# Half of a down projection computed by Strassen's seven products of quarters in a two-layer decoder kernel

## The chip, the cores and the metric

The kernel runs on one core of one Trainium2 chip (trn2). The number of interest is the time of one execution on the device, in microseconds (us). Smaller is better. Beside the times of plain runs there is one execution under the hardware profiler, with a trace of every instruction; durations in this text are from that trace.

The core has a matmul engine (TensorE, PE in the profile; its loads of the stationary operand are listed apart as PEld), a vector engine (VectorE, DVE), a scalar engine (ScalarE, ACT), GpSimd (POOL) and SyncE (SP), which here only issues DMAs. Each engine works through its own queue in order. Matmuls write to PSUM, which has eight banks of 128 x 512 fp32 values here.

## The reference

Two decoder layers on 256 tokens of 1024 features, in float32: a token mixer (forgetting attention in layer 0, block-sparse attention in layer 1), then a SwiGLU feed-forward network (FFN) with 2816 inner features, then a gated per-layer input. The change lies in the FFN alone:

```python
u = _rmsnorm(h, ffn_norm_g[i])
gu = u @ ffn_w_in[i]
h = h + (jax.nn.silu(gu[..., :D_FF]) * gu[..., D_FF:]) @ ffn_w_out[i]
```

The last product is the down projection: (256 tokens x 2816) times (2816 x 1024).

## The kernel before

Activations are held with features on the 128 partitions and the 256 tokens along the free axis. A product in float32 precision is made of three matmuls in a faster 32-bit type (fp32r): every operand x is split into hi = x rounded to fp32r and lo = x - hi, and `mm3` adds hi·hi, hi·lo and lo·hi into one PSUM region. So each weight tile takes a step on ScalarE (`whi`, a copy that rounds, L186) and one on VectorE (`wlo`, a subtraction, L187) after its DMA has filled `raw`. Weights come in blocks of 128 x 1024, numbered in the order of their use (`raw82` is the 83rd); they lie in DRAM in that order. `raw`, `whi` and `wlo` each have a ring of six buffers.

`half` and `blocks` fetch and split one block; `blocks` puts it APART = 16 columns (64 bytes) behind the start of its tile. At some calls `blocks` gets a "form", which shifts the first one or two of its eight 128 x 128 pieces by eight columns (`_BOTH1`, `_BOTH2`, used at `AGAIN`, for instance: up with f = 4 and f = 12) and the rest by 64.

`ffn` goes through 22 row blocks f of 128 inner features:

- `up([f])` takes two weight blocks (gate and up) and makes 2 x 8 x 3 = 48 matmuls into a bank `gu`: stationary operand a 128 x 128 piece of the weights, moving operand 256 columns of the normalized activations `g`.
- `gated` reads that bank on VectorE (`gut`, L610), takes Silu on ScalarE, multiplies (L613) and splits the product into `fh` and `fl` (L301, L302).
- `down(f)` takes one weight block (128 rows x 1024 columns) and makes 8 x 3 = 24 matmuls into four banks `fo` (`acc`): two banks for each half `hf` of the output features. Stationary operand a piece of the weights, moving operand `fh` or `fl`.

The loop runs in pairs: up(f), up(f+1), down(f-2), down(f-1). The last four row blocks are taken by `last`, one half of the output after the other, so that the first half is finished early: it is added to the residual `hx` (its tile is named `gx` in the profile) by `residual(0, ...)` while the second is still running. Between them stands `ple_up` (`pu`), the up product of the per-layer input; in layer 1 its roles are swapped (stationary activations, moving weights), and `by_token` adds f32 transposes (`tp`).

The code is written in program order, and a scheduler then places each instruction in its engine's queue: a split is moved ahead of work whose operands come later, so VectorE and ScalarE run some blocks ahead of TensorE. What limits this lead is the rings: a split waits until TensorE has finished with the block that had its buffer, and a load until VectorE has split the block that was there.

Of the kernel before, what the change touches and what calls it, by code (L numbers as in the profile page):

```python
# [10 lines left out]
F32 = mybir.dt.float32  # L11
F32R = mybir.dt.float32r
# [9 lines left out]
NP = H // 2  # L22
DFF = 2816
FT = DFF // P
DP = 256
EPS = 1e-6
BUCKETS = 32
# [52 lines left out]
def trunk(ctx: ExitStack, tc: tile.TileContext, pt, w, cst, gf, out):  # L80
# [7 lines left out]
    def bank(name):  # L88
        return ps.tile([P, 512], F32, tag="bank", name=name)
# [52 lines left out]
    def half(at=0, entry=0, form=None):  # L142
# [38 lines left out]
        for q in range(parts):  # L181
# [4 lines left out]
            nc.scalar.activation(hi[:, c], raw[:, c], AF.Copy)  # L186
            nc.vector.tensor_tensor(lo[:, c], raw[:, c], f32(hi[:, c]), op=ALU.subtract)  # L187
        return hi, lo

    def blocks(entry=False, form=None):  # L190

# [375 lines left out]
        nf.square(0)  # L567

    def ffn(layer, nm, filler, np_):
        acc = []  # L570
        prod = {}

        def up(fs):

            bks = {f: bank(f"gu{layer}_{f}") for f in fs}

            def step(f, a, wt, k, start):
                o = bks[f][:, a * S:(a + 1) * S]
                if f == a == k == 0:
                    for n, (w_, x) in enumerate(((wt[0][k], nm.k(k)[0]), (wt[1][k], nm.k(k)[0]), (wt[0][k], nm.k(k)[1]))):  # L580
                        mm(o, w_, x, start=n == 0, stop=False, skip_group_check=True)
                else:
                    mm3(o, (wt[0][k], wt[1][k]), nm.k(k), start, k == KT - 1)

            if fs[0] == 0:
                wts = {f: (blocks(form=_BOTH2 if f == 0 else None), blocks()) for f in fs}
                for k in range(KT):
                    if k == 3:
                        nm.turn(1)
                        nm.square(1)  # L590
                    if k == 6:
                        table(AF.Abs_reciprocal_sqrt, nm.ss[:, 0:1])
                    for f in fs:
                        for a in range(2):
                            step(f, a, wts[f][a], k, k == 0 and a == 0)
                nm.root()
                table(AF.Silu, nm.y)
                return fs, bks
            for a in range(2):
                wt = blocks(form=_BOTH1 if (fs[0], a) in AGAIN else None)  # L600
                for k in range(KT):
                    if (fs[0], a, k) == (2, 0, 4):
                        gated(*early)
                    step(fs[0], a, wt, k, k == 0)
            gated(fs, bks)

        def gated(fs, bks):
            for f in fs:
                t = work.tile([P, 2, S], F32, tag="t2k", bufs=3, name=f"gut{layer}_{f}")
                nc.vector.tensor_tensor(t, bks[f].rearrange("p (a s) -> p a s", s=S), nm.rows(), op=ALU.mult)  # L610
                sg = work.tile([P, S], F32, tag="sg", name=f"sg{layer}_{f}")
                nc.scalar.activation(sg, t[:, 0], AF.Silu)
                nc.vector.tensor_tensor(sg, sg, t[:, 1], op=ALU.mult)  # L613
                th = work.tile([P, S], F32R, tag="th", bufs=4, name=f"fh{layer}_{f}")
                tl = work.tile([P, S], F32R, tag="tl", bufs=4, name=f"fl{layer}_{f}")
                split(th, tl, sg)
                prod[f] = th, tl

        def down(f, wt):
            for hf in range(2):  # L620
                feature_unit(acc[hf], wt, 4 * hf, prod[f], f == 0, False)

        def last(f, hf):

            wt = blocks(form={(FT - 2, 0): _BOTH1, (FT - 2, 1): _BOTH1}.get((f, hf)) if layer else None)
            for i in range(2):
                feature_unit(acc[hf], wt, 4 * i, prod[f + i], False, f + i == FT - 1)

        early = up([0, 1])
        for f in range(2, FT, 2):  # L630
            up([f])
            up([f + 1])
            if layer == 0 and f in (6, 8, 10, 12):
                moba[0](f // 2 - 3)
            if f == FT - 6:
                pp = filler()
            if f == 2:
                acc.extend([bank(f"fo{layer}_{hf}_{t}") for t in range(2)] for hf in range(2))
            if f < FT - 2:
                down(f - 2, blocks())  # L640
                down(f - 1, blocks())
        last(FT - 4, 0)
        filler(pp)
        last(FT - 2, 0)
        residual(0, acc[0])
        last(FT - 4, 1)
        np_.turn(0)
        if layer == 0:
            np_.square(0)
        else:  # L650
            by_token(np_, 0)
        last(FT - 2, 1)
        residual(1, acc[1])
# [224 lines left out]
    return t.reshape(2, P, HC).transpose(1, 0, 2).reshape(P, HW)  # L878


def _buckets():
# [78 lines left out]
```

## Time and profile before

| | us |
|---|---|
| median of 3 runs (lowest, highest) | 641.54 (641.27, 641.66) |
| the profiled execution | 641.68 |
| its span, first to last instruction | 639.9 |
| VectorE splits of weight blocks (L187), 198 of them | 237.1 busy |
| ScalarE roundings of weight blocks (L186), 198 | 205.1 busy |

The page's first line gives each engine's busy time and share of the span; a second part cuts the span into 40 slices; a third follows the chain of work that ended last back from the last instruction. Of the answers of the trace, the timeline lists instructions by start (us from the span's start), duration, engine, line, operation, tiles (out<-in) and shape; a row that ends in x8 is eight in a row. The table by windows gives, for stretches of the span, each engine's busy time and number of instructions. TensorE's matmuls overlap: one that is listed with 0.28 us may be followed by the next after 0.11 us, so the spacing of their starts is what counts.

### The profile page before, as it was taken

The numbers are of one execution on the slowest core, as the hardware profiler recorded it, in microseconds if no ns is written. First come the engines' busy times: TensorE is split into PE (matmuls) and PEld (weight loads), VectorE is DVE, ScalarE is ACT, GpSimd is POOL, SyncE is SP. The second block draws the span as 40 slices with busy tenths as digits, with TensorE's granted clock in tenths as the row PEclk, the third lists the DMA queues.
The fourth block names the chain that finished last, engine by engine and source line by source line (L and its number), as shares of the span: only waits on it lengthen the run. The fifth ranks groups of instructions, "written<-read, shape, count | busy, mean of one in ns | idle before, by whom it ended". The sixth has DMA issues, their size and how long they took to land.

```text
span 639.9 us, 13124 instructions
## 1 busy us (share of the span) xinstructions
PE 632.8 (99%) x5300; PEld 611.9 (96%) x5300; DVE 459.2 (72%) x798; ACT 379.4 (59%) x667; POOL 16.3 (3%) x33
## 2 busy tenths in 40 slices
PE   9999999999999999999999999999999999999996
PEld 7899999999999999999989999999999999999985
DVE  6987985886666666658996687678766666666765
ACT  7857675864444445448876486558444444454672
POOL 2500000000000000000000000000000000000002
PEclk9999999999999999999999999999999999999999
DMA  9889744376666666665687544435866566566501
GB/s 333 299 268 362 241 151 148 111 257 198 195 196 196 196 195 206 190 192 167 212 274 261 174 161 149 132 100 180 251 196 198 197 198 194 189 205 194 192 1 66
DMA packets 37212, 125.18 MB, mean 196 GB/s; under 512 B 3968, under 2 KB 7072, under 8 KB 37152
## 3 DMA queue, kind: packets, MB, share of 16 engines
q1 hardware_dynamic: 36832, 123.91, 59.7%
q8 instruction: 41, 0.67, 0.4%
q10 hardware_dynamic: 320, 0.44, 0.2%
q14 instruction: 19, 0.16, 0.1%
HBM read 123.25 MB, written 4.24 MB: 199 GB/s over the span
## 4 chain that ended last, share of the span: by engine, by line
PE 98%; POOL 0%; issue 0%; DVE 0%; ACT 0%; POOLq 0%; DVEq 0%
PE gu L100 12%; PE gu L98 12%; PE gu L99 12%; PE fo L100 6%; PE fo L98 6%; PE fo L99 6%; PE pq L98 5%; PE pq L99 5%; PE pq L100 5%; PE wo L98 2%; PE wo L99 2%; PE wo L100 2%; PE pg L99 2%; PE pg L100 2%; PE pg L98 2%; PE v L98 2%
## 5 line engine op out<-in xcount | busy, mean ns | idle before, releaser
L187 DVE TENSOR_TENSOR wlo<-raw,whi 128x1024 fp32r<-128x1024 f32 (+1 forms) x198 | 237.1, 1202 | 103.8 <-ACT whi L186 101.7
L186 ACT ACTIVATE whi<-raw 128x1024 fp32r<-128x1024 f32 (+1 forms) x198 | 205.1, 1041 | 146.8 <-issue 55.5
L99 PE MATMUL gu<-g,whi 128*128 128x256 f32 x702 | 193.8, 276 | 0.0
L98 PE MATMUL gu<-g,whi 128*128 128x256 f32 x702 | 193.8, 276 | 0.0
L100 PE MATMUL gu<-g,wlo 128*128 128x256 f32 x702 | 193.8, 276 | 0.0
L100 PEld LDWEIGHTS gu<-g,wlo 128*128 128x128 f32 x702 | 131.8, 188 | 0.0
L99 PEld LDWEIGHTS gu<-g,whi 128*128 128x128 f32 x702 | 131.8, 188 | 0.0
L98 PEld LDWEIGHTS gu<-g,whi 128*128 128x128 f32 x702 | 131.8, 188 | 0.0
L98 PE MATMUL fo<-fh,whi 128*128 128x256 f32 x352 | 97.3, 276 | 0.0
L100 PE MATMUL fo<-fh,wlo 128*128 128x256 f32 x352 | 97.2, 276 | 0.0
L99 PE MATMUL fo<-fl,whi 128*128 128x256 f32 x352 | 97.2, 276 | 0.0
L98 PE MATMUL pq<-g,whi 128*128 128x256 f32 x256 | 71.1, 278 | 0.0
L100 PE MATMUL pq<-g,wlo 128*128 128x256 f32 x256 | 70.8, 276 | 0.0
L99 PE MATMUL pq<-g,whi 128*128 128x256 f32 x256 | 70.7, 276 | 0.0
L98 PEld LDWEIGHTS fo<-fh,whi 128*128 128x128 f32 x352 | 66.1, 188 | 0.0
L99 PEld LDWEIGHTS fo<-fl,whi 128*128 128x128 f32 x352 | 66.1, 188 | 0.0
L100 PEld LDWEIGHTS fo<-fh,wlo 128*128 128x128 f32 x352 | 66.1, 188 | 0.0
L98 PEld LDWEIGHTS pq<-g,whi 128*128 128x128 f32 x256 | 48.0, 188 | 1.1 <-issue 0.7
L301 ACT ACTIVATE fh<-sg 128x256 fp32r<-128x256 f32 x44 | 18.1, 416 | 51.6 <-DVE sg L613 51.6
L99 PEld LDWEIGHTS pq<-g,whi 128*128 128x128 f32 x256 | 48.1, 188 | 0.1
L100 PEld LDWEIGHTS pq<-g,wlo 128*128 128x128 f32 x256 | 48.0, 188 | 0.0
L162 ACT ACTIVATE whi<-raw 128x256 fp32r<-128x256 f32 (+3 forms) x44 | 25.4, 623 | 24.0 <-PE pq L99 6.6
(179 smaller groups left out, 984.3 us busy)
## 6 DMA issues: line engine op xcount, KB each, us to landing
raw<-w SPq DMA_DIRECT2D x212, 512.0 KB, 4.2
d<-d SPq DMA_DIRECT2D x4, 768.0 KB, 9.4
raw<-w SPq DMA_DIRECT2D x8, 256.0 KB, 4.5
bias<-d SPq DMA_DIRECT2D x4, 512.0 KB, 7.4
bias<-cd SPq DMA_DIRECT2D x2, 768.0 KB, 8.0
gx<-w SPq DMA_DIRECT2D x1, 512.0 KB, 5.2
bias<-cd SPq DMA_DIRECT2D x1, 512.0 KB, 7.8
p<-pt SPq DMA_DIRECT2D x2, 256.0 KB, 4.3
```

What stands on the lines that cost most here:

```text
L98: mm(o, ah, bh, start=start, stop=False, skip_group_check=True)
L99: mm(o, ah, bl, start=False, stop=False, skip_group_check=True)
L100: return mm(o, al, bh, start=False, stop=stop, skip_group_check=True).ins
L162: nc.scalar.activation(o, raw[:, c], AF.Copy)
L186: nc.scalar.activation(hi[:, c], raw[:, c], AF.Copy)
L187: nc.vector.tensor_tensor(lo[:, c], raw[:, c], f32(hi[:, c]), op=ALU.subtract)
L301: nc.scalar.activation(hi, src, AF.Copy)
```

## The change

For the first 512 output columns (the first half) and the first 18 row blocks (SEVEN = 22 - 4) the down projection is done by Strassen's scheme. A pair of row blocks gives a product of two 2 x 2 matrices of quarters: the activations (two halves of 128 tokens by two row blocks) times the weights (two row blocks by two groups of 256 columns). It takes seven products of quarters where the plain way takes eight, and for them sums of quarters on both sides.

- Weights: `sevenfold` loads the pair's first half as one block (its four quarters in the order that `_quarters` packs), makes four sums on VectorE (`sums`, L197 to L199) in a tile of the `raw` ring, and splits three quarters (128 x 768) and the four sums (128 x 1024). So a pair now takes seven places of each ring, not six. These tiles are used from their start, without APART.
- Activations: `gated` keeps the pair's product in `tt`, and `differences` makes four differences (`dif`, L649 to L651) and splits them into `dh` and `dl`.
- `products`: seven times three matmuls into the four banks `fs` (`seven`), with roles swapped: stationary operand 128 tokens of `fh`, `fl`, `dh` or `dl`, moving operand 256 weight columns. The second half (`acc[1]`) is done as before, with one block for both row blocks.
- After the 18th row block `combined` adds the seven sums (a copy of one bank on ScalarE, five additions on VectorE, tile `c`). The result has tokens on the partitions, so `turned` transposes it (eight 128 x 128 f32 transposes on TensorE into `fc`) between up(20) and up(21) and adds it to the residual. The first half's `acc[0]` starts only with row block 18.

During the loop six PSUM banks are held for sums (four before), so two are left for `gu` (four before). Everything outside the FFN keeps its instructions.

```diff
+SEVEN = FT - 4
...
+    def sevenfold():
...
+        raw, more = [work.tile([P, 4, S], F32, tag="raw", bufs=RAW, name=f"{n}{i}") for n in ("raw", "sums")]
+        nc.sync.dma_start(raw, packed(w, w_at(i), HW))
+        nc.vector.tensor_tensor(more[:, 0:2], raw[:, 1:3], raw[:, 0:1].to_broadcast([P, 2, S]), op=ALU.add)
+        nc.vector.tensor_tensor(more[:, 2], more[:, 0], raw[:, 2], op=ALU.add)
+        nc.vector.tensor_tensor(more[:, 3], more[:, 2], raw[:, 3], op=ALU.add)
+        got = []
+        for q, src in enumerate((raw[:, 1:4], more[:, 0:4])):
+            n = 3 + q
+            hi, lo = [work.tile([P, HW + 2 * LINE], F32R, tag=f"w{x}", bufs=6, name=f"w{x}{i}_{q}")[:, 0:n * S]
+                      .rearrange("p (n s) -> p n s", s=S) for x in ("hi", "lo")]
+            split(hi, lo, src)
+            got += [(hi[:, j], lo[:, j]) for j in range(n)]
+        return got
...
-                th = work.tile([P, S], F32R, tag="th", bufs=4, name=f"fh{layer}_{f}")
-                tl = work.tile([P, S], F32R, tag="tl", bufs=4, name=f"fl{layer}_{f}")
+                th = work.tile([P, S], F32R, tag="e", bufs=6, name=f"fh{layer}_{f}")
+                tl = work.tile([P, S], F32R, tag="pt", bufs=6, name=f"fl{layer}_{f}")
                 split(th, tl, sg)
                 prod[f] = th, tl
-
-        def down(f, wt):
-            for hf in range(2):
-                feature_unit(acc[hf], wt, 4 * hf, prod[f], f == 0, False)
+                if f < SEVEN and f % 2:
+                    differences(f // 2)
+
+        def differences(i):
+            q = quarters.pop(i).rearrange("p k (t s) -> p (k t) s", s=P)
+            d = work.tile([P, 4, P], F32, tag="tt", bufs=3, name=f"dif{layer}_{i}")
+            nc.vector.tensor_tensor(d[:, 0:2], q[:, 2:3].to_broadcast([P, 2, P]), q[:, 0:4:3], op=ALU.subtract)
+            nc.vector.tensor_tensor(d[:, 2], q[:, 3], d[:, 0], op=ALU.subtract)
+            nc.vector.tensor_tensor(d[:, 3], q[:, 1], d[:, 2], op=ALU.subtract)
+            dh, dl = [work.tile([P, 4, P], F32R, tag="qkt", bufs=4, name=f"d{x}{layer}_{i}") for x in "hl"]
+            split(dh, dl, d)
+            diff[i] = dh, dl
+
+        def products(i):
+            b11, b22, b21, x1, x2, x3, x4 = sevenfold()
...
+            for o, at, new, a, b in ((m52, 1, 1, a21, b11), (m43, 0, 1, a22, b21), (m43, 1, 0, a3, b22), (m52, 0, 0, a11, x2),
+                                     (m1, 0, 1, a1, x3), (m76, 1, 1, a6, x1), (m76, 0, 0, a7, x4)):
+                mm3(o[:, at * S:(at + 1) * S], a, b, bool(new) and i == 0, i == SEVEN // 2 - 1)
...
+            nc.scalar.activation(m, m43, AF.Copy)
...
+        def down(f):
+            products(f // 2)
+            wt = blocks()
+            for i in range(2):
+                feature_unit(acc[1], wt, 4 * i, prod[f + i], f + i == 0, False)
...
             up([f])
+            if f > SEVEN:
+                turned(c)
             up([f + 1])
...
             if f < FT - 2:
-                down(f - 2, blocks())
-                down(f - 1, blocks())
+                down(f - 2)
+            if f == SEVEN:
+                c = combined()
```

What the scheduler makes of it is shown at three places in layer 0. The first is TensorE at the first down, right behind up(3). Before, in the first bank `fo0_0_0`, the first two of eight products of row block 0 with weight block 40:

```order
L98 MATMUL fo0_0_0_1809<-fh0_0_1675,whi40_1814 128x256
L99 MATMUL fo0_0_0_1809<-fl0_0_1676,whi40_1814 128x256
L100 MATMUL fo0_0_0_1809<-fh0_0_1675,wlo40_1815 128x256
L98 MATMUL fo0_0_0_1809<-fh0_0_1675,whi40_1814 128x256
L99 MATMUL fo0_0_0_1809<-fl0_0_1676,whi40_1814 128x256
L100 MATMUL fo0_0_0_1809<-fh0_0_1675,wlo40_1815 128x256
```

In the change, from the second of the seven products on: `fs0_0` is the bank m43, `fs0_2` m52, `fs0_1` m1; `w..40_0` are quarters of the weights, `w..40_1` sums of them:

```order
L99 MATMUL fs0_0_1823<-whi40_0_1835,fh0_1_1683 128x256
L100 MATMUL fs0_0_1823<-wlo40_0_1836,fh0_1_1683 128x256
L101 MATMUL fs0_0_1823<-whi40_0_1835,fl0_1_1684 128x256
L99 MATMUL fs0_0_1823<-whi40_0_1835,dh0_0_1691 128x256
L100 MATMUL fs0_0_1823<-wlo40_0_1836,dh0_0_1691 128x256
L99 MATMUL fs0_2_1825<-whi40_1_1839,fh0_0_1675 128x256
L100 MATMUL fs0_2_1825<-wlo40_1_1840,fh0_0_1675 128x256
L101 MATMUL fs0_2_1825<-whi40_1_1839,fl0_0_1676 128x256
L101 MATMUL fs0_0_1823<-whi40_0_1835,dl0_0_1692 128x256
```

The operands have changed places, `dh0_0` is needed from the seventh matmul on, and the first matmul with `dl0_0` has been put three places back, behind a product that needs neither.

The second place is VectorE ahead of these products, from the reading of up(2)'s bank on. Before:

```order
L610 TENSOR_TENSOR gut0_2_1730<-gu0_2_1651,row1_1644 128x512
L302 TENSOR_TENSOR fl0_0_1676<-sg0_0_1672,fh0_0_1675 128x256
L302 TENSOR_TENSOR fl0_1_1685<-sg0_1_1681,fh0_1_1684 128x256
L167 TENSOR_TENSOR wlo42_1876<-raw42_1874,whi42_1875 128x128
L167 TENSOR_TENSOR wlo42_1876<-raw42_1874,whi42_1875 128x896
L613 TENSOR_TENSOR sg0_2_1732<-sg0_2_1732,gut0_2_1730 128x256
L187 TENSOR_TENSOR wlo43_1908<-raw43_1906,whi43_1907 128x1024
```

And with the change, up to the split `dl0_0`:

```order
L629 TENSOR_TENSOR gut0_2_1737<-gu0_2_1651,row1_1644 128x512
L321 TENSOR_TENSOR fl0_0_1676<-tt0_0_1672,fh0_0_1675 128x256
L321 TENSOR_TENSOR fl0_1_1684<-tt0_0_1672,fh0_1_1683 128x256
L649 TENSOR_TENSOR dif0_0_1687<-tt0_0_1672 128x256
L188 TENSOR_TENSOR wlo41_1866<-raw41_1864,whi41_1865 128x1024
L650 TENSOR_TENSOR dif0_0_1687<-tt0_0_1672,dif0_0_1687 128x128
L637 TENSOR_TENSOR tt0_2_1739<-tt0_2_1739,gut0_2_1737 128x256
L651 TENSOR_TENSOR dif0_0_1687<-tt0_0_1672,dif0_0_1687 128x128
L168 TENSOR_TENSOR wlo42_1897<-raw42_1895,whi42_1896 128x128
L168 TENSOR_TENSOR wlo42_1897<-raw42_1895,whi42_1896 128x896
L321 TENSOR_TENSOR dl0_0_1692<-dif0_0_1687,dh0_0_1691 128x512
```

The same work has the differences, the half block 41 and the wait for `dh0_0` between it, and `dl0_0` stands last.

The third is VectorE in the steady part of the loop, around the reading of up(14)'s bank. Before:

```order
L187 TENSOR_TENSOR wlo77_3053<-raw77_3051,whi77_3052 128x1024
L187 TENSOR_TENSOR wlo78_3084<-raw78_3082,whi78_3083 128x1024
L610 TENSOR_TENSOR gut0_14_2942<-gu0_14_2881,row1_1644 128x512
L187 TENSOR_TENSOR wlo79_3114<-raw79_3112,whi79_3113 128x1024
L613 TENSOR_TENSOR sg0_14_2944<-sg0_14_2944,gut0_14_2942 128x256
L302 TENSOR_TENSOR fl0_14_2948<-sg0_14_2944,fh0_14_2947 128x256
L187 TENSOR_TENSOR wlo80_3154<-raw80_3152,whi80_3153 128x1024
L610 TENSOR_TENSOR gut0_15_3012<-gu0_15_2951,row1_1644 128x512
```

With the change, from the split of a set of sums on (`sums76`, of pair 12) to the sums of the next (`sums82`, made from `raw82`):

```order
L321 TENSOR_TENSOR wlo76_1_3120<-sums76_3110,whi76_1_3119 128x1024
L321 TENSOR_TENSOR dl0_6_2893<-dif0_6_2888,dh0_6_2892 128x512
L188 TENSOR_TENSOR wlo77_3146<-raw77_3144,whi77_3145 128x1024
L197 TENSOR_TENSOR sums82_3328<-raw82_3327 128x512
L629 TENSOR_TENSOR gut0_14_3023<-gu0_14_2962,row1_1644 128x512
L188 TENSOR_TENSOR wlo78_3177<-raw78_3175,whi78_3176 128x1024
L637 TENSOR_TENSOR tt0_14_3025<-tt0_14_3025,gut0_14_3023 128x256
L198 TENSOR_TENSOR sums82_3328<-sums82_3328,raw82_3327 128x256
L199 TENSOR_TENSOR sums82_3328<-sums82_3328,raw82_3327 128x256
L321 TENSOR_TENSOR fl0_14_3029<-tt0_14_3025,fh0_14_3028 128x256
```

The first addition on `raw82` now stands between the splits and the reading of the bank; `raw82` is loaded to where `sums76` was, so its load can be issued only when the first row shown is done.

More of the change, by code (lines that the diff above doesn't have):

```diff
@@ L569, in ffn @@
     def ffn(layer, nm, filler, np_):
-        acc = []
-        prod = {}
+        acc, seven = {}, []
+        prod, quarters, diff = {}, {}, {}
         def up(fs):
@@ L610, in gated @@
                 nc.vector.tensor_tensor(t, bks[f].rearrange("p (a s) -> p a s", s=S), nm.rows(), op=ALU.mult)
-                sg = work.tile([P, S], F32, tag="sg", name=f"sg{layer}_{f}")
+                if f >= SEVEN:
+                    sg = work.tile([P, S], F32, tag="sg", name=f"sg{layer}_{f}")
+                else:
+                    if f % 2 == 0:
+                        quarters[f // 2] = work.tile([P, 2, S], F32, tag="tt", bufs=3, name=f"tt{layer}_{f}")
+                    sg = quarters[f // 2][:, f % 2]
@@ new lines, in products @@
+        def products(i):
+            b11, b22, b21, x1, x2, x3, x4 = sevenfold()
+            (a11, a21), (_, a22) = [[[x[:, t * P:(t + 1) * P] for x in prod[2 * i + k]] for t in range(2)] for k in range(2)]
+            a3, a7, a1, a6 = [[x[:, n] for x in diff[i]] for n in range(4)]
+            m43, m1, m52, m76 = seven
+            for o, at, new, a, b in ((m52, 1, 1, a21, b11), (m43, 0, 1, a22, b21), (m43, 1, 0, a3, b22), (m52, 0, 0, a11, x2),
+                                     (m1, 0, 1, a1, x3), (m76, 1, 1, a6, x1), (m76, 0, 0, a7, x4)):
+                mm3(o[:, at * S:(at + 1) * S], a, b, bool(new) and i == 0, i == SEVEN // 2 - 1)
@@ new lines, in combined @@
+        def combined():
+            m43, m1, m52, m76 = [b.rearrange("p (a s) -> p a s", s=S) for b in seven]
+            m = work.tile([P, 2, S], F32, tag="t2k", bufs=3, name=f"m43_{layer}")
+            nc.scalar.activation(m, m43, AF.Copy)
+            c = work.tile([P, 4, S], F32, tag="bias", bufs=1, name=f"c{layer}")
+            nc.vector.tensor_tensor(c[:, 2], m[:, 0], m52[:, 1], op=ALU.add)
+            nc.vector.tensor_tensor(c[:, 1], m[:, 1], m52[:, 0], op=ALU.add)
+            o = c[:, 0:4:3]
+            nc.vector.tensor_tensor(o, m, m52, op=ALU.subtract)
+            nc.vector.tensor_tensor(o, o, m1[:, 0:1].to_broadcast([P, 2, S]), op=ALU.add)
+            nc.vector.tensor_tensor(o, o, m76, op=ALU.add)
+            return c.rearrange("p (t n) s -> p t (n s)", n=2)
@@ new lines, in turned @@
+        def turned(c):
+            bks = [bank(f"fc{layer}_{b}") for b in range(2)]
+            for m in range(4):
+                for t in range(2):
+                    nc.tensor.transpose(bks[m // 2][:, (m % 2) * S + t * P:(m % 2) * S + (t + 1) * P],
+                                        c[:, t, m * P:(m + 1) * P], ident)
+            residual(0, bks)
+        def down(f):
[3 more added lines that the diff above has]
+                feature_unit(acc[1], wt, 4 * i, prod[f + i], f + i == 0, False)
@@ L637, in ffn @@
             if f == 2:
-                acc.extend([bank(f"fo{layer}_{hf}_{t}") for t in range(2)] for hf in range(2))
+                seven.extend(bank(f"fs{layer}_{t}") for t in range(4))
+                acc[1] = [bank(f"fo{layer}_1_{t}") for t in range(2)]
             if f < FT - 2:
-                down(f - 2, blocks())
-                down(f - 1, blocks())
+                down(f - 2)
+            if f == SEVEN:
+                c = combined()
+        acc[0] = [bank(f"fo{layer}_0_{t}") for t in range(2)]
         last(FT - 4, 0)
```

10 lines of the change are left out of this document (7 added, 3 removed).

## The prediction

> **What bounds the kernel now.** I read the page first, its busy line, the slices of the granted clock and the chain that ended last:
>
> ```profile
> PE 632.8 (99%) x5300; PEld 611.9 (96%) x5300; DVE 459.2 (72%) x798; ACT 379.4 (59%) x667; POOL 16.3 (3%) x33
> PEclk9999999999999999999999999999999999999999
> PE 98%; POOL 0%; issue 0%; DVE 0%; ACT 0%; POOLq 0%; DVEq 0%
> ```
>
> TensorE is busy for 632.8 of 639.9 us at full clock, and the chain is TensorE for 98%. A "busy" TensorE says little, so I looked at the starts of its matmuls in the timeline of one pair of row blocks: the first matmul of gu (up), of fo (down) and of the next gu. Then at the same stretch in the table by windows (length, PE busy, instructions, clock, DMA share, GB/s), and at most of layer 0's FFN there, all engines (PE, PEld, DVE, ACT, POOL):
>
> ```profile
> 172.00 0.28 PE L98 MATMUL gu<-g,whi 128*128 128x256 f32 x1
> 182.88 0.28 PE L98 MATMUL fo<-fh,whi 128*128 128x256 f32 x1
> 188.32 0.28 PE L98 MATMUL gu<-g,whi 128*128 128x256 f32 x1
> ...
> 172.00:188.32 16.32, 16.32 (x147) 1.00 0.64 196
> ...
> 139.33:290.00 150.67, 150.67 (x1331) 150.67 (x1330) 94.79 (x112) 72.64 (x97) 0.00 (x0) 1.00 0.64 201
> ```
>
> A pair is 96 matmuls of gu in 10.88 us and 48 of fo in 5.44 us: 0.1133 us from start to start in both, with no hole. So in this stage the time is the number of TensorE instructions times their spacing; VectorE (63%) and ScalarE (48%) lie beside it. Three things can move the end: the number, the spacing, and a new hole.
>
> **What is removed.** Each pair loses a block of three matmuls out of 24 (seven products for eight), in nine pairs of each of two layers: 54 matmuls x 0.1133 = **6.12 us** off the path.
>
> **Turning back.** 16 transposes are new on TensorE (eight in each layer), within up's work. The trace has eight f32 transposes of the same shape amid fo:
>
> ```profile
> 606.21 1.03 PE L701 MATMUL tp<-cs,gx 128*128 128x128 f32 x8
> 607.00 0.36 PE L98 MATMUL fo<-fh,whi 128*128 128x256 f32 x1
> 607.21 0.28 PE L99 MATMUL fo<-fl,whi 128*128 128x256 f32 x1
> ```
>
> From 606.21 to 607.21 stand these eight and one fo matmul; less the latter's 0.113 that is 0.89 us, and some 0.03 for settling: 2 x 0.92 = **+1.84 us**, with 0.05 each way. The Trainium skill ("TensorE: Matmul & The Clock Gate", Part 4: PE-mode transpose) speaks against the change here: about 275 ns a transpose in a kernel's context. By that figure the 16 would take 4.4 us and the whole sum would end 2.6 us later, at an estimated 644.1; the rows give about 0.11 us each, so the trace does not agree.
>
> **The spacing of the products.** In gu and fo the stationary operand is a weight block, set 16 columns (64 bytes) off its tile's start (APART), and the moving one an activation at its tile's start. In the products the roles are swapped and both lie at a start or at whole steps of 512 bytes from it. The nearest rows are pu's and pu_own's 256-wide matmuls, which have the same roles and no offset either; and the wo stretch, which has the old offset and still another spacing:
>
> ```profile
> 600.15 0.28 PE L99 MATMUL pu<-wlo,phi 128*128 128x256 f32 x1
> ...
> 600.75 0.28 PE L98 MATMUL fo<-fh,whi 128*128 128x256 f32 x1
> ...
> 601.34 0.28 PE L100 MATMUL fo<-fh,wlo 128*128 128x256 f32 x1
> ...
> 632.72 0.28 PE L98 MATMUL pu_own<-u,phi 128*128 128x256 f32 x1
> ...
> 633.30 0.28 PE L100 MATMUL pu_own<-u,plo 128*128 128x256 f32 x1
> ...
> 96.00 0.28 PE L98 MATMUL wo<-o,whi 128*128 128x256 f32 x1
> ...
> 96.59 0.29 PE L100 MATMUL wo<-o,wlo 128*128 128x256 f32 x1
> ```
>
> pu: five in 0.60 us, 0.120 each. pu_own: five in 0.58, 0.116. I take 0.118. For 2 x 9 x 21 = 378 products that is 378 x 0.0047 = **+1.8 us** over the old spacing; the ends are 0 (as gu) and +2.5 (all as pu). On the way back from pu the first five fo matmuls took 0.59 (600.75 to 601.34), 0.024 over the old spacing; that settling comes 18 times: **+0.4 us** (0 to 1).
>
> The Trainium skill (same page, Part 2: What happens when you issue a matmul) has a rule by which no such term exists: the moving operand and the weight load each have their own read port, and loading the next weights takes nothing from the running matmul. By it the placement would cost nothing and the sum would be that of the first rival below; pu's 0.120 against gu's 0.113 does not agree.
>
> **The work beside it.** Durations on VectorE overlap, so I take start to start:
>
> ```profile
> 178.68 1.22 DVE L187 TENSOR_TENSOR wlo<-raw,whi 128x1024 fp32r<-128x1024 f32 x1 [0.34 <-ACT whi L186]
> 179.82 0.42 DVE L613 TENSOR_TENSOR sg<-sg,gut 128x256 f32<-128x256 f32 x1
> ...
> 108.81 1.28 DVE L328 TENSOR_TENSOR gx<-gx,wo 128x512 f32<-128x512 f32 x2
> ...
> 130.05 0.75 DVE L613 TENSOR_TENSOR sg<-sg,gut 128x256 f32<-128x256 f32 x2
> ...
> raw<-w SPq DMA_DIRECT2D x212, 512.0 KB, 4.2
> ```
>
> 1024 elements: 1.14; 512: 1.28 less 0.68 = 0.60; 256: 0.33; hence 0.87 for 768 and 0.20 for 128. A pair now costs VectorE 6 x 1.14 + 2 x 0.60 (gut) + 4 x 0.33 = 9.36 us. New per pair: the split of 768 (0.87), sums (0.60 + 0.33 + 0.33), differences (0.33 + 0.20 + 0.20) and their split (0.60), together 3.46: 12.82 of the pair's 15.98 us (141 x 0.1133). ScalarE gains 768 and 512 elements. Both stay beside TensorE. What is queued in order matters more: "sums" takes a place in the ring of six raw tiles, and the load of the next quarters (raw82) goes where sums76 was, so it is issued only when wlo76_1 is done, 4.2 us before it lands; but the first addition on raw82 stands three rows behind wlo76_1, and gut14 and all later splits are queued behind it. The loop from one such split to the next: load 4.2; then 0.60 + 0.60 + 1.14 + 0.33 + 2 x 0.33 + 0.33 + 1.14 for the rest of block 14, 0.60 + 1.14 + 0.33 + 1.14 + 0.33 for 15, and 0.33 + 0.87 + 0.40 + 1.22 up to the end of the split: 11.1 + 4.2 = 15.3 us, some 15.7 with the handovers. TensorE's 15.98 is just longer. VectorE idles some 2 us a pair for the load, and the splits stay ahead: wlo84 stands in the queue before gut17, which waits for the end of w81, and TensorE still has w82 and w83 (about 5 us) before it needs w84. Cost 0; with that cover gone, rival three.
>
> **The first products.** Here the cover is short. TensorE comes to down(0) at 133.88, and now it needs the differences' split, behind much else on VectorE:
>
> ```profile
> 127.71 1.29 DVE L610 TENSOR_TENSOR gut<-gu,row 128x512 f32<-128x512 f32 x2
> 128.91 1.22 DVE L187 TENSOR_TENSOR wlo<-raw,whi 128x1024 fp32r<-128x1024 f32 x1
> ...
> 133.88 0.28 PE L98 MATMUL fo<-fh,whi 128*128 128x256 f32 x1
> ```
>
> gut0 and gut1 end about 128.8 as before (of the three splits ahead of them the last is now a 768). Then in the new order: wlo40_1 1.14, two multiplications 0.66, gut2 0.60, two fl 0.66, differences 0.73 with wlo41 1.14 and a multiplication 0.33 between, wlo42 1.2, dl0 0.69: 7.15 us, so dl0 is there at 136.0. ScalarE's dh0 comes after the last difference (134.1), a 256 and a 512, near 135.0. TensorE does six matmuls (to 134.56), waits 0.45, does five (135.57), waits 0.45: about 1.0 with the semaphores. Layer 1 starts alike: **+2.0 us** (0.8 to 3). From then on the lead grows, since up brings 10.9 us of TensorE before the next products.
>
> **The end of the sums.** combined() waits for the last products. VectorE has two splits, a multiplication, an fl and five additions (2 x 0.33 + 3 x 0.60) before c: about 8 us after w87, and TensorE comes to the transposes 2.5 + 2.72 + 5.44 = 10.6 us after it. ScalarE's copy of m43 waits for the products too, with whi93 and fh19 queued behind it, which TensorE needs only after the transposes. Cost 0 (up to 1 in each layer if a load is late).
>
> **The sum.** -6.12 + 1.84 + 1.8 + 0.4 + 2.0 = -0.1 us on the profiled execution's 641.68 (span 639.9 and 1.8 around it), which is 0.14 above the median of the runs shown. Forecast: **641.5 us**, its own range 639.8 to 643.5. About 0.2% (1.3 us) is what a measurement can tell from no change.
>
> **The rivals.**
> 1. *The products run at gu's spacing* and the return settles at once: -6.12 + 1.84 + 2.0 = -2.3, **639.3**. For it: at the very first 256-wide pu matmul (600.04 to 600.15) the step was still 0.11. Against: the five after it.
> 2. *The slow spacing stays after the products* (the other side). wo shows that a stretch with the old offset can stay at 0.118 (five in 0.59 at 96.00, up to the stretch's end). If fo comes out of the products in this state, gu goes on in it, until something sets it off again: the first block that AGAIN shifts at f = 4 and 12, or the next products. Per layer nine fo of 24, six up pairs of 96 and the 48 before the transposes: 840 matmuls, x 2 x 0.0047 = +7.9, less the 0.4 of settling: **649.0**; some pairs alone give 644 to 648. For it: layer 1's fo at 600.75 came back quickly, but with its first block shifted, which down's blocks() does not ask for. Against: gu, fo and pu change places elsewhere without a trace of it. It decides against the change from a fifth of these matmuls on.
> 3. *VectorE's loop with the load becomes the bound*, if loads take over 5 us: each 0.3 us over the 15.98 eats the lead of some 5 us, and what is left past that in nine pairs twice is +1 to +5: **644**.
> 4. *The first products' wait is hidden too* and the spacing is gu's: **637.4**.
>
> **How the numbers follow.** Forecast 0.42, rival one 0.22, two 0.25, three 0.06, four 0.05. Range 638.8 to 648.5: it holds the forecast, nearly all of rival one, three and most of two, and takes in the unknown spacing from 0 to +2.5 and the wait from 0.8 to 3. Faster by over 0.2%: 0.06 of the forecast, 0.20 of rival one, and four: 0.31. Within: 0.28 and 0.02: 0.30. Slower: 0.08, two and three: 0.39.
>
> **What would show it.** The starts of fs matmuls in a pair well inside: 21 in 2.38 us (rival one) or 2.5; the first gu after the products 0.113 or 0.118 (rival two). In layer 0 a hole on TensorE ahead of the first dh matmul, released by ScalarE, and one ahead of the first dl. fc: eight in about 0.9, without a hole before. VectorE idle ahead of the first addition of sums, ended by the load, but no idle TensorE at whi or wlo inside the stage. I am wrong if TensorE waits there, or if fo and gu change their spacing.

## The result, and the profile after

| | median (us) | lowest to highest | runs |
|---|---|---|---|
| before, beside it | 641.6 | 641.27 to 642.12 | 4 |
| the change | 649.86 | 649.36 to 650.46 | 4 |

The ratio is 1.0128 (95% interval 1.0111 to 1.0146): **slower by 1.3%**, 8.4 us above the forecast and beyond its range. The profiled execution took 649.79 us, its span 648.0.

The page of the change, busy line, slices of the granted clock, chain:

```profile
PE 640.0 (99%) x5262; PEld 617.9 (95%) x5262; DVE 521.5 (80%) x956; ACT 405.3 (63%) x705; POOL 16.3 (3%) x33
PEclk9999999999999999999999999999999999999998
PE 91%; DVE 5%; DMA 1%; issue 1%; ACT 1%; POOL 0%; POOLq 0%; DVEq 0%
```

TensorE has 38 instructions fewer (5300 to 5262: 54 out, 16 in), its busy time is 7.2 us longer, the clock is the same. Fewer instructions and more time means a wider spacing, so again the starts decide. TensorE's timeline of the change, at the borders of one pair inside the stage: the last matmul of gu, the first and the last of fs, the first of fo, and where the next gu begins:

```profile
167.69 0.28 PE L101 MATMUL gu<-g,wlo 128*128 128x256 f32 x1
167.81 0.28 PE L99 MATMUL fs<-whi,fh 128*128 128x256 f32 x1
...
170.21 0.28 PE L101 MATMUL fs<-whi,dl 128*128 128x256 f32 x1
170.32 0.28 PE L99 MATMUL fo<-fh,whi 128*128 128x256 f32 x1
```

The table by windows of the change, cut at such borders (length, busy and instructions of PE, PEld, DVE, ACT, POOL, then clock, DMA share, GB/s; neighbours that reach over a border are counted too): the 96 gu ahead of these products, the 21 products, the 24 fo behind them, and the 96 gu at f = 12:

```profile
156.50:167.81 11.31, 11.31 (x99) 11.31 (x98) 8.87 (x14) 5.38 (x7) 0.00 (x0) 1.00 0.62 202
167.81:170.32 2.51, 2.51 (x23) 2.51 (x22) 2.48 (x5) 2.09 (x3) 0.00 (x0) 1.00 0.65 199
170.32:173.15 2.83, 2.83 (x27) 2.83 (x25) 2.83 (x8) 1.50 (x3) 0.00 (x0) 1.00 0.58 193
206.46:217.36 10.90, 10.90 (x99) 10.90 (x97) 8.02 (x13) 5.29 (x7) 0.00 (x0) 1.00 0.54 188
```

The products step by 0.120 us (2.51 / 21), fo behind them by 0.118 (2.83 / 24), and gu by 0.118 too (11.31 / 96), where it was 0.1133 before. Inside the loop only gu at f = 4 and f = 12, whose first block AGAIN shifts, goes back (10.90 for 96), until the next products. That is rival two. Behind the transposes the two layers differ: in layer 0 gu went back to the quick step without a shifted block (the 47 matmuls behind the first took 5.34 us, 0.114 each), in layer 1 it stayed at 0.118 (5.53). The clock is 1.00 in all of these.

TensorE's waits in the change, and the timeline at the two places in layer 0:

```profile
PE gu L600 <- DVE g L234: 0.5, 2, 0.2
PE fs L101 <- DVE dl L321: 0.4, 2, 0.2
```

```profile
111.83 0.29 PE L600 MATMUL gu<-g,wlo 128*128 128x256 f32 x1
112.35 0.39 PE L600 MATMUL gu<-g,whi 128*128 128x256 f32 x1 [0.24 <-DVE g L234]
112.58 0.28 PE L99 MATMUL gu<-g,whi 128*128 128x256 f32 x1
...
134.76 0.28 PE L101 MATMUL fs<-whi,fl 128*128 128x256 f32 x1
135.11 0.39 PE L99 MATMUL fs<-whi,dh 128*128 128x256 f32 x1
...
135.69 0.28 PE L101 MATMUL fs<-whi,fl 128*128 128x256 f32 x1
136.14 0.39 PE L101 MATMUL fs<-whi,dl 128*128 128x256 f32 x1 [0.17 <-DVE dl L321]
...
278.32 1.04 PE L685 MATMUL fc<-cs,c 128*128 128x128 f32 x8
279.11 0.36 PE L99 MATMUL gu<-g,whi 128*128 128x256 f32 x1
279.32 0.28 PE L100 MATMUL gu<-g,whi 128*128 128x256 f32 x1
```

The steps are 0.52 and 0.23 at the first gu, 0.35 ahead of dh, 0.45 ahead of dl, each of the latter two with a second step of 0.22 behind it. The wait at gu was not in the prediction: the first addition of `sums` stands on VectorE ahead of a residual addition, and the splits of g, which TensorE needs, are queued behind.

Steps from start to start, added up over all TensorE rows of the two traces, give the whole account (us):

```
                                   before    after   difference
54 matmuls fewer, at 0.1133                            -6.1
fs, spacing over 0.1133 (378)                          +2.4
fo, spacing over before's (624)                        +2.1
gu, spacing (2112 matmuls)                             +5.7
first products, waits                                  +1.6
first gu, waits                                        +1.05
fc, 16 transposes and the step behind                  +1.8
sum                                                    +8.5
gu in all                          239.62   246.59     +6.97
fo and fs in all                   119.84   119.70     -0.14
```

Added up before rounding, the differences give 8.4 (6.97 - 0.14 + 1.58 for the 16 transposes themselves). The spans differ by 8.1, since the first matmuls of the program, which wait for loads, took 0.2 less in the execution after.

### The profile page after: what moved, and what is told of

It reads as the page before. It is cut to its first block, busy times and chain, and to the rows that moved or that the text cites. A ratio compares the mean times of both kernels' runs of the same rounds, so it can differ in the third digit from the quotient of the medians.

```text
span 648.0 us, 13258 instructions
## 1 busy us (share of the span) xinstructions
PE 640.0 (99%) x5262; PEld 617.9 (95%) x5262; DVE 521.5 (80%) x956; ACT 405.3 (63%) x705; POOL 16.3 (3%) x33
## 4 chain that ended last, share of the span: by engine, by line
PE 91%; DVE 5%; DMA 1%; issue 1%; ACT 1%; POOL 0%; POOLq 0%; DVEq 0%
PE gu L100 12%; PE gu L101 11%; PE gu L99 11%; PE pq L99 5%; PE pq L101 4%; PE pq L100 4%; PE fo L100 4%; PE fo L99 4%; PE fo L101 4%; PE fs L101 2%; PE fs L99 2%; PE fs L100 2%; PE pg L101 2%; PE pg L100 2%; PE pg L99 2%; PE v L99 2%
## 5 line engine op out<-in xcount | busy, mean ns | idle before, releaser
L188 DVE TENSOR_TENSOR wlo<-raw,whi 128x1024 fp32r<-128x1024 f32 (+1 forms) x180 | 214.4, 1196 | 51.3 <-ACT whi L187 49.4
L187 ACT ACTIVATE whi<-raw 128x1024 fp32r<-128x1024 f32 (+1 forms) x180 | 184.9, 1036 | 101.2 <-PE gu L100 32.7
L99 PE MATMUL gu<-g,whi 128*128 128x256 f32 x702 | 196.2, 279 | 0.0
L100 PE MATMUL gu<-g,whi 128*128 128x256 f32 x702 | 196.0, 279 | 0.0
L99 PE MATMUL fo<-fh,whi 128*128 128x256 f32 x208 | 58.3, 280 | 0.0
L101 PE MATMUL fo<-fh,wlo 128*128 128x256 f32 x208 | 58.2, 280 | 0.0
L100 PE MATMUL fo<-fl,whi 128*128 128x256 f32 x208 | 58.2, 280 | 0.0
L99 PEld LDWEIGHTS fo<-fh,whi 128*128 128x128 f32 x208 | 39.7, 191 | 0.0
L101 PEld LDWEIGHTS fo<-fh,wlo 128*128 128x128 f32 x208 | 39.1, 188 | 0.0
L100 PEld LDWEIGHTS fo<-fl,whi 128*128 128x128 f32 x208 | 39.1, 188 | 0.0
L168 DVE TENSOR_TENSOR wlo<-raw,whi 128x256 fp32r<-128x256 f32 (+3 forms) x44 | 29.3, 683 | 8.9 <-ACT whi L163 8.8
```

Source lines behind the costliest of these rows:

```text
L99: mm(o, ah, bh, start=start, stop=False, skip_group_check=True)
L100: mm(o, ah, bl, start=False, stop=False, skip_group_check=True)
L101: return mm(o, al, bh, start=False, stop=stop, skip_group_check=True).ins
L168: nc.vector.tensor_tensor(t[:, a + b0 * P:a + b1 * P], raw[:, b0 * P:b1 * P], f32(ht[:, a0:a0 + (b1 - b0) * P]), op=ALU.subtract)
```

## The experiments

Theory A: the spacing is set by how the stationary and the moving operand lie to each other; the products leave TensorE in a slow spacing that stays, and a shifted first block ends it. Theory B: the heavier traffic of VectorE and ScalarE beside TensorE slows it. The kernel of before beside the runs had medians of 641.25 to 641.6.

| run | median (us) | lowest to highest | ratio to before (95%) |
|---|---|---|---|
| e1_kick | 647.05 | 645.15 to 648.53 | 1.0093 (1.0076 to 1.0109) |
| e2_apart | 648.06 | 647.92 to 648.79 | 1.0103 (1.0088 to 1.0118) |
| e3_both | 648.10 | 644.6 to 649.71 | 1.0094 (1.006 to 1.0128) |
| e4_flat | 670.18 | one run | |
| e5_ring | 647.94 | 646.38 to 651.77 | 1.0109 (1.0073 to 1.0146) |
| e6_ringonly | 650.37 | 649.94 to 650.51 | 1.0137 (1.012 to 1.0154) |
| e7_start | 648.07 | 646.66 to 648.36 | 1.0098 (1.0083 to 1.0113) |
| e8_step | 651.42 | 648.41 to 652.26 | 1.0146 (1.0121 to 1.0172) |
| e10_queue | 642.80 | 642.65 to 643.26 | 1.0022 (1.0012 to 1.0033) |
| e11_all | 640.45 | 640.2 to 641.32 | 0.999 (0.9981 to 1.0) |
| e12_first | 639.49 | 639.41 to 639.8 | 0.9971 (0.996 to 0.9982) |
| e13_stat | 638.75 | 638.57 to 639.43 | 0.996 (0.9947 to 0.9974) |

### The spacing: e1 to e4

e1, against the change:

```diff
         def down(f):
             products(f // 2)
-            wt = blocks()
+            wt = blocks(form=_BOTH1)
```

> The change, with the first block of fo behind each pair's products read shifted, in the form that AGAIN gives up's blocks at f = 4 and 12 (one argument in down). Nothing else differs. Theory A, rival two of the prediction (the products leave TensorE in a slow spacing, and a shifted block sets it off again): fo and gu step by 0.113 us again in nearly all pairs, the products stay at 0.120, and the time falls by about 840 x 2 x 0.0045 = 7.6 less some 18 x 0.03 for settling, from 649.9 to 642.8 (641.8 to 644). Theory B (what VectorE and ScalarE now read and write beside TensorE slows its matmuls, so the spacing follows the load and not an order of addresses): no change, fo and gu at 0.118, 649.9 within 0.7.

e1, the same three stretches by windows (gu, products, fo):

```profile
156.33:167.21 10.88, 10.88 (x98) 10.88 (x97) 8.79 (x15) 5.48 (x8) 0.00 (x0) 1.00 0.60 201
167.21:169.73 2.52, 2.52 (x23) 2.52 (x22) 2.48 (x5) 1.86 (x3) 0.00 (x0) 1.00 0.53 176
169.73:172.47 2.74, 2.74 (x26) 2.74 (x25) 2.74 (x7) 1.72 (x3) 0.00 (x0) 1.00 0.60 185
```

gu is at 0.1133 again (10.88 / 96), fo at 0.114 with its settling, the products unchanged, with VectorE and ScalarE as busy as before the edit. The spacing did what A says and B does not. The time did not: 2.8 us less instead of 7.1, and its executions lie 3.4 us apart. TensorE had a new wait in layer 1:

```profile
PE fc L685 <- DVE c L677: 2.1, 1, 2.1
PE fs L101 <- DVE dl L321: 1.2, 2, 0.6
```

The first of these stands ahead of the transposes, for the last of `combined`'s additions, and takes back part of the gain. The profiled execution, at 645.15, is the fastest of the four.

e2, against the change (e3 is e1 and e2 together):

```diff
-            hi, lo = [... name=f"w{x}{i}_{q}")[:, 0:n * S]
+            hi, lo = [... name=f"w{x}{i}_{q}")[:, 3 * APART:3 * APART + n * S]
```

> The change, with the split quarters in whi and wlo (the products' moving operand) set 48 columns off the tile's start; pg_own reads an operand with that offset at 0.113 us in the trace. Nothing else differs. Theory A (spacing is set by where the two operands lie): the products step by 0.113 instead of 0.120: 378 x 0.0066 = 2.5 us less, 647.4. If products that run at the quick spacing also leave fo and gu in it, another 7.6: 639.8. Between these two A alone doesn't decide. Theory B (load of the other engines): no change, 649.9 within 0.7.

> Both edits together: the products' moving operand 48 columns off its tile's start, and the first block of fo behind them shifted. Theory A: products, fo and gu all at 0.113 us: 649.9 - 2.5 - 7.6 + 0.5 = 640.3 (639 to 642). Theory B: no change, 649.9 within 0.7.

e2 by windows: products behind a quick gu, fo, slow gu, products behind that:

```profile
151.29:153.77 2.48, 2.48 (x24) 2.48 (x22) 2.42 (x5) 2.34 (x3) 0.00 (x0) 1.00 0.87 274
153.77:156.59 2.82, 2.82 (x26) 2.82 (x25) 2.82 (x6) 1.25 (x3) 0.00 (x0) 1.00 0.84 296
156.59:167.90 11.31, 11.31 (x98) 11.31 (x97) 8.92 (x14) 5.38 (x7) 0.00 (x0) 1.00 0.61 192
167.90:170.31 2.41, 2.41 (x24) 2.41 (x22) 2.38 (x4) 1.99 (x3) 0.00 (x0) 1.00 0.58 201
```

With the offset the products have two spacings too: 0.118 behind a quick gu (2.48 / 21) and 0.115 with settling behind a slow one (2.41 / 21); fo behind them was slow either way. The time fell by 1.8 of the 2.5 named. In e3 fo and gu came back as in e1 but for two stretches of layer 0, which stayed at 0.118 (fo behind the first products, and all from the transposes to the end of its fo), and the wait for c grew to 3.7 us: 640.3 was missed mainly for the same reason as in e1.

e4, against the kernel of before, both places in `blocks`:

```diff
-            return half(APART, 0, form)
-        hi, lo = half(APART, ENTRY * P if entry else 0)
+            return half(0, 0, form)
+        hi, lo = half(0, ENTRY * P if entry else 0)
```

> The kernel of before, no products, with every weight block at its tile's start instead of 16 columns behind it (the form that AGAIN shifts stays shifted). The placement alone, under the old load of VectorE and ScalarE. Theory A: gu, fo and wo step by 0.118 to 0.120 us over most of their length; some 4000 matmuls x 0.005 to 0.0066 = 20 to 26 us slower than before, less what the shifted blocks win back, so 655 to 668. Theory B: no change from 641.6, within 1.

e4 by windows, 48 fo and the 96 gu behind them:

```profile
172.60:178.36 5.76, 5.76 (x51) 5.76 (x49) 3.90 (x5) 2.73 (x4) 0.00 (x0) 1.00 0.60 185
178.36:189.88 11.52, 11.52 (x99) 11.52 (x97) 6.36 (x7) 4.85 (x6) 0.00 (x0) 1.00 0.56 182
```

0.120 us a matmul, without a single product, with the light VectorE of before, and 28.6 us slower in all (one execution). The offset alone makes that difference; B cannot. It is the same 0.120 as that of the products in the change. The time lies 2 us above the expected range, which counted on the shifted blocks to win something back: here they did not, gu at f = 4 took 0.120 too.

### What eats the gain: e5 to e8, e10

In e1 the first addition of each pair's sums waits on VectorE for its load. VectorE's timeline of e1, these rows alone:

```profile
179.50 0.69 DVE L197 TENSOR_TENSOR sums<-raw 128x512 f32<-128x512 f32 x1 [0.70 <-DMA raw<-w]
195.58 0.69 DVE L197 TENSOR_TENSOR sums<-raw 128x512 f32<-128x512 f32 x1 [1.83 <-DMA raw<-w]
212.42 0.69 DVE L197 TENSOR_TENSOR sums<-raw 128x512 f32<-128x512 f32 x1 [2.50 <-DMA raw<-w]
229.64 0.69 DVE L197 TENSOR_TENSOR sums<-raw 128x512 f32<-128x512 f32 x1 [3.53 <-DMA raw<-w]
246.22 0.69 DVE L197 TENSOR_TENSOR sums<-raw 128x512 f32<-128x512 f32 x1 [2.88 <-DMA raw<-w]
```

From one to the next (179.50 to 246.22 in four pairs) are 16.68 us; TensorE in e1 takes 10.88 + 2.52 + 2.74 = 16.14 a pair. So VectorE falls behind by half a us a pair. In the change TensorE's 11.31 + 2.51 + 2.83 = 16.65 just covers it.

That is not all of e1's wait for c. It came in layer 1 alone, though layer 0 has the same loop. In layer 1 ScalarE also stands still for the load of u (weights of the per-layer input, needed later), and there the next rounding, for which VectorE then waits 3.39 us, is queued behind it. ScalarE's timeline at u, in e1 and then in e10, which follows below:

```profile
576.85 0.63 ACT L320 ACTIVATE u<-u 128x512 fp32r<-128x512 f32 x1 [3.61 <-DMA u<-w]
```

```profile
584.82 0.64 ACT L321 ACTIVATE u<-u 128x512 fp32r<-128x512 f32 x1 [1.12 <-DMA u<-w]
```

e5 is e1 with the sums in a tile of their own; e6 has that edit alone:

```diff
-        raw, more = [work.tile([P, 4, S], F32, tag="raw", bufs=RAW, name=f"{n}{i}") for n in ("raw", "sums")]
+        raw, more = [work.tile([P, 4, S], F32, tag=tag, bufs=b, name=f"{n}{i}") for n, tag, b in (("raw", "raw", RAW), ("sums", "bias", 1))]
```

> The change with fo's first block shifted as in the run e1_kick, and besides the tile that holds the sums moved out of the ring of six raw tiles into the space that is free between the attention's bias and c, so that no load of weights waits for a split of sums. In e1_kick the spacing came back as theory A says, but TensorE waited 2.1 us in layer 1 for c, and the lead of the splits over their first use fell by 0.3 to 2 us a pair once a pair took 16.1 us. Theory L (VectorE's loop with the load through the ring takes 16.5 us or more a pair, not the 15.3 to 15.7 of the prediction, so it eats what TensorE gains): without that loop the lead stays at 8 us or more, no wait for c, 643.0 (642.3 to 643.8) with executions within 1 us. Rival U (the late load of u in layer 1, with the splits queued behind it on ScalarE, makes that wait by itself): the lead may stay, but a wait of 1 us or more ahead of fc in layer 1 remains, 645 to 648.

> The change with nothing but the sums' own tile as in the run e5_ring; fo isn't shifted. Theory A with L: TensorE at 0.118 us takes 16.65 us a pair and hides the loop, so nothing moves: 649.9 within 0.7. If part of what the change lost was the ring, the time falls by that part, and the forecast's cost of 0 for the loop was wrong in this kernel already.

e6 moved nothing, as A with L had it. e5 did not move either: 647.94 with a wait of 2.3 us at c is what U named, not L. But neither run tests the loop, since the addition's idle time was as large as before (21.9 us in e6). That the loop is hidden in the change is seen from the change's own trace, where TensorE has no wait inside the stage once the first products are past. All 18 of these additions in the change, in e1 and in e5 (the row by line, then the idle time ahead of them and its count):

```profile
L197 DVE TENSOR_TENSOR sums<-raw x18: 680/692/693, 109.5 to 563.0; 128x512 f32<-128x512 f32 x18
...
  DMA raw<-w: 17.4, 12
```

```profile
L197 DVE TENSOR_TENSOR sums<-raw x18: 678/691/693, 109.4 to 559.2; 128x512 f32<-128x512 f32 x18
...
  DMA raw<-w: 23.2, 12
```

```profile
L197 DVE TENSOR_TENSOR sums<-raw x18: 678/692/695, 109.2 to 558.2; 128x512 f32<-128x512 f32 x18
...
  DMA raw<-w: 24.5, 13
```

With the freer ring the scheduler put the addition one row earlier, and it still stood ahead of its load.

e5's trace shows a second cost of such a wait. Behind it the granted clock fell to 0.50 for some 3 us, and matmuls stepped by 0.21. By windows, from 591.57 on:

```profile
591.57:594.77 3.20, 3.20 (x16) 3.20 (x16) 3.20 (x6) 0.42 (x1) 0.00 (x0) 0.50 0.89 302
```

The traces of e3, e7 and e8 have such a stretch behind each wait for c of 2.3 us or more (3.3 to 3.9 there). e1's, with a wait of 2.1, has none. A stretch like this costs about 1.5 us (15 steps of 0.21 in place of 0.1133, an estimate from e5's rows). It may be why executions of these kernels lie up to 5.4 us apart: e1's profiled one had a mean granted clock of 0.997, its three slower ones 0.995.

e7 mends the starts:

```diff
-                nc.vector.tensor_tensor(self.ss, self.ss, sq, op=ALU.add)
+                self.added = nc.vector.tensor_tensor(self.ss, self.ss, sq, op=ALU.add).ins
...
-        nc.vector.tensor_tensor(more[:, 0:2], raw[:, 1:3], raw[:, 0:1].to_broadcast([P, 2, S]), op=ALU.add)
+        with tc.issue_after(behind) if behind is not None else nullcontext():
+            nc.vector.tensor_tensor(more[:, 0:2], raw[:, 1:3], raw[:, 0:1].to_broadcast([P, 2, S]), op=ALU.add)
...
-                    differences(f // 2)
+                    with nullcontext() if f > 1 else tc.high_priority():
+                        differences(f // 2)
...
-            b11, b22, b21, x1, x2, x3, x4 = sevenfold()
+            b11, b22, b21, x1, x2, x3, x4 = sevenfold(None if i else nm.added)
```

> e5_ring, with two changes of order on VectorE at the start of each FFN: the additions of the first sums stand behind the sums of squares instead of ahead of the residual and g's splits, and the first differences ahead of fl0 and fl1. That removes the waits that the profile of the change shows there: 0.41 and 0.11 at the first matmuls of gu, and 0.23 + 0.11 and 0.34 + 0.11 at the first products, about 1.3 a layer. If these waits are costs of their own: e5_ring less 2.6, so 640.4 if that gives 643.0. If something behind them is as late (the first loads), less than 1 of it shows.

The waits at both starts were gone from its trace, and the wait for c grew from 2.3 to 3.9 us: the gain ahead of the loop was given back behind it, and e5's time did not fall (648.07). e8, on top of e7, has the products' moving operand at `3 * APART + 8 - 8 * q` (q = 0 the quarters, q = 1 the sums):

> e7_start, with the products' moving operand 48 columns off its tile's start for the four sums (as in e2_apart) and 56 for the three quarters, a step of 8 columns at the products' fourth factor and at their first. In e2_apart products that came behind a slow gu ran at 0.114 and behind a quick one at 0.118. If the step sets them off as the shifted block does in gu: products at 0.113 to 0.114, 378 x 0.006 = 2.3 less than e7_start, about 638. If not: 0.118, 0.7 less.

Its products stayed at 0.118 and it was slower, not quicker: layer 0 now waited for c as well (3.3 us, and 3.7 in layer 1). e10 is e1 with one order given, that of the additions in VectorE's queue (by the `issue_after` of e7):

```diff
-                nc.vector.tensor_tensor(sg, sg, t[:, 1], op=ALU.mult)
+                done[f] = nc.vector.tensor_tensor(sg, sg, t[:, 1], op=ALU.mult).ins
...
-            b11, b22, b21, x1, x2, x3, x4 = sevenfold()
+            b11, b22, b21, x1, x2, x3, x4 = sevenfold(done[2 * i + 1] if i else None)
```

> e1_kick with one change of order: the additions of a pair's sums stand on VectorE behind the pair's last multiplication (tt of the odd row block) instead of ahead of gut of the even one. Nothing else, and the sums stay in the ring of raw tiles. In e1_kick and e5_ring VectorE stands idle for 2.1 to 2.4 us a pair at the first of these additions, until the quarters have landed, while gut, whose gu is long done, and the splits are queued behind it; the lead of the splits falls by 0.8 to 1 us a pair and layer 1 ends with TensorE waiting for c. Theory H (that place in the queue makes the loop): no idle VectorE at that addition, the lead stays above 6 us, no wait for c, 643.1 (642.3 to 644) with executions within 1 us. Rival W (VectorE and ScalarE have too much work for 16.1 us a pair, whatever the order): the lead still falls, 645 or more.

e10, the same additions, and VectorE's timeline at two of them and the next gut:

```profile
L198 DVE TENSOR_TENSOR sums<-raw x18: 681/685/693, 109.5 to 566.4; 128x512 f32<-128x512 f32 x18
...
  DMA raw<-w: 0.5, 2
```

```profile
220.31 0.69 DVE L198 TENSOR_TENSOR sums<-raw 128x512 f32<-128x512 f32 x1
...
236.45 0.69 DVE L198 TENSOR_TENSOR sums<-raw 128x512 f32<-128x512 f32 x1
...
242.84 0.69 DVE L630 TENSOR_TENSOR gut<-gu,row 128x512 f32<-128x512 f32 x1 [0.51 <-PE gu L101]
```

0.5 us of idle time instead of 23.2, 16.14 us from one to the next, and VectorE waits for TensorE, not the other way. No wait for c, 642.80 of the 643.1 named, executions within 0.6. W (too much work) does not hold, and in this loop H does. U is not settled: with the new order the scheduler also moved u (the second of the two rows above), 8 us later and behind the roundings that stood behind it in e1, and it waits 1.1 us for 3.6. In e8's layer 0 a wait for c came without any u; how e1's 2.1 us divide between loop and u was not tested.

### Together: e11 to e13

> e7_start (shifted first block of fo, the sums' own tile, the order at the start of each FFN) with the order of e10_queue. Theory H: no wait for c, no wait at the first gu and the first products (e7_start's profile has none left), so e10_queue less 2.4: 640.7 (639.8 to 641.8), even with the kernel of before. Rival W: 644 or more.

640.45: 2.35 less than e10; in the traces the stretches at the two starts are 2.6 shorter. The seven products now break even with the kernel of before. e12 offsets the products' moving operand and sets b11 eight columns further:

```diff
+            for j0, j1, at in ((0, 1, 3 * APART + 8), (1, 3, 3 * APART + LINE)) if q == 0 else ((0, n, 3 * APART),):
```

> e11_all, with the products' moving operand 48 columns off its tile's start and the first factor of the seven (b11) 8 columns further, in its own split: what sets gu off, tried on the products. If it does: products at 0.113 instead of 0.120, 378 x 0.0066 = 2.5 less than e11_all, 638.2. If not, as in e8_step: 0.118, 0.7 less; the two splits more per pair may cost the lead.

639.49, 1.0 less, and the products at 0.118: not set off. e13 shifts a stationary factor instead (moving operand at 3 * APART throughout):

```diff
+            for n0, n1, at in ((0, 1, FURTHER), (1, 4, LINE)):
+                dh, dl = [b[:, at + n0 * P:at + n1 * P].rearrange("p (n s) -> p n s", s=P) for b in both]
+                split(dh, dl, d[:, n0:n1])
```

> e11_all, with the products' moving operand 48 columns off its tile's start and the third factor on the stationary side (a3, first of the differences) 8 columns off the place of the other three: what is shifted in gu and fo is the stationary operand, in e12_first it was the moving one, and there the products stayed at 0.118 from the fourth matmul to the last. If a shifted stationary operand sets them off: some ten of the 21 of a pair, behind a3 and a few of settling, at 0.113: 18 x 10 x 0.0045 = 0.8 less than e12_first, 638.7. If not: 0.118 throughout, 639.5 as e12_first (within 0.4).

e13, products of one pair: the first, the first on the shifted a3 (dh), the second on a11 four matmuls later, the last, and fo:

```profile
182.37 0.28 PE L99 MATMUL fs<-whi,fh 128*128 128x256 f32 x1
...
183.08 0.28 PE L99 MATMUL fs<-whi,dh 128*128 128x256 f32 x1
...
183.56 0.28 PE L100 MATMUL fs<-wlo,fh 128*128 128x256 f32 x1
...
184.69 0.28 PE L101 MATMUL fs<-whi,dl 128*128 128x256 f32 x1
184.81 0.28 PE L99 MATMUL fo<-fh,whi 128*128 128x256 f32 x1
```

Up to 183.56 ten steps take 1.19 us (0.119), from there ten take 1.13 (0.113). Ten of 21 came back, as named, and the time is 638.75 of 638.7: 0.4% below before.

## Why the prediction was wrong

- **The step that failed** is the term "+0.4 us" for settling back, with the "Against" of rival two. It took the way back from `fo` in layer 1 (five slow matmuls), whose first block is shifted, as the way back of down's fo, whose first block is not. The prediction says so itself in rival two, and still gave the quick return more weight. The runs showed that fo and gu go on at 0.118 until something sets them off: the term measured +7.8 (2.1 in fo, 5.7 in gu), and e1's shift alone removed all but some 0.7 of it. That "gu, fo and pu change places elsewhere without a trace of it" was no evidence: between gu and fo no operand changes sides, and the shifted blocks stand where it would have shown.
- **The spacing of the products**: 0.120 rather than 0.118, +2.4 for +1.8, inside its ends. e4 shows the cause that the prediction only argued. The Trainium skill ("TensorE: Matmul & The Clock Gate", Part 2: What happens when you issue a matmul) has two independent read ports and says that loading the next weights takes nothing from the running matmul. The prediction read that as a rule by which no placement would cost anything, and so read it does not agree with e4: 0.120 against 0.1133 with nothing but an offset taken away.
- **The removed matmuls and the transposes** were right: 54 fewer; fc took 0.79 up to the next start plus a step of 0.21 where 0.113 would stand, 0.89 a layer for 0.92, with no hole ahead. One point of the working does not hold: the Trainium skill (same page, Part 4: PE-mode transpose) gives about 275 ns as the duration of one transpose (measured there with bf16), and the trace agrees, since the row of eight lasts 1.04 us and seven steps of 0.109 leave 0.27 for the last. The prediction took the figure as the time from one to the next, and so found a disagreement.
- **The first products**: right in place and order, 0.8 a layer for 1.0.
- **Not foreseen**: the wait at the first gu, +0.5 a layer. The order of the queues showed the first addition of sums ahead of the residual; the prediction looked at sums only inside the loop.
- **VectorE's loop**: cost 0 was right for the change, by luck. The loop takes 16.7 us, not 15.3 to 15.7, which is more than the forecast's own pair of 15.98; it stayed hidden because TensorE was slow. With a TensorE near the forecast's, something like rival three comes: e1 is that case, at 647.05, though u has a part in it. The place was right (the first addition queued ahead of its load, gut and the splits behind it) and the sum was too small. In one turn of the change's loop the work from the addition (230.18) to the end of the split of sums (241.98) took 11.8 us for 11.1, and from there the next addition (246.94) came 4.96 later, for 4.2.
- **The end of the sums**: cost 0 held in the change.

The likeliest case gave 641.5, rival two 649.0. The mechanism of the larger loss stood in the prediction, with its price; the chance of 0.25 was too small, and a range that ends at 648.5 leaves out that rival's own 649.0. That its 7.9 came so near to the 7.8 measured is partly luck: the step widened by 0.0045, not 0.0047, and 48 gu and 24 fo behind the transposes of layer 1, which it did not count, were slow as well.

## What to carry to other kernels

Where TensorE is the bound and does nothing but matmuls, count the steps between starts, not the busy time, and look at the first stretch behind any change of roles: a slow spacing can go on in work that nobody touched. A return that was seen counts only for the same code, first block included. When a repaired step gives back less than it should, look for the engine that it had covered: here an addition that stood in a queue ahead of its load. Ordering it behind later work was worth 4 us, with the move of u that came along. And a wait of TensorE can cost more than its length: look at the granted clock behind it.

## What the runs showed of the hardware

At a granted clock of 1.00 and the same shape (128 x 128 stationary, 256 columns moving), most matmuls of these stages start 0.1133, 0.118 or 0.120 us apart. 0.120 came where no operand had the offset of 16 or 48 columns (fs in the change; gu and fo in e4, shifted blocks included). With one operand 16 or 48 columns off there are two lasting spacings, 0.1133 and 0.118. Which one holds depends on what ran before, and the slow one went on through the 120 matmuls (24 fo, 96 gu) up to the next products. In e2 the same products ran at 0.118 behind a quick gu and at 0.115 behind a slow one. Three things bear on it:

- A first piece of the stationary operand eight columns off brought the quick one back after some four matmuls, in fo (e1, behind all 18 products; in e3 behind 17) and in the products (e13). The same shift of the moving operand did not (e12).
- Where fo's first block is not shifted, the products left it slow, without an offset of their own (the change) and with one (e2).
- A row of eight transposes could turn it either way: from 0.118 to 0.1133 in layer 0 of the change, from 0.1133 to 0.118 in layer 1 of e1; in layer 1 of the change it left the slow one as it was.

Why was not found out. Behind stops of TensorE of 2.3 us or more the traces of e3, e5, e7 and e8 have a granted clock of 0.50 for some 3 us, behind e1's 2.1 us none.
